# Feed-forward part of an encoder step: sums of x1 on VectorE alone, weight rounding on ScalarE, and another bank for the second half product

## The chip, the cores and the metric

One core of a Trainium2 chip runs the whole program in one launch. The metric is the device time of that launch in microseconds, as the median of several runs. Beside the plain runs one execution was recorded by the hardware profiler; its rows are quoted below. Engines go by the names of the profile: PE (TensorE), DVE (VectorE), ACT (ScalarE), POOL (GpSimd), SP (SyncE, which issues the DMAs).

## The reference, cut to what matters

One layer of a streaming encoder: four parallel token mixers, an output projection with a layer norm, and a gated convolutional feed-forward part. Prompt (1024 tokens) and sample (64 tokens) share the weights. D_MODEL is 1024, D_FF 2048, everything in float32. The change lies in the last five lines of the layer:

```python
x1 = layer_norm(DN_ALPHA * x + jnp.einsum('btd,de->bte', mix, w_out), ln1_g, ln1_b)
gate_pre = jnp.einsum('btd,df->btf', x1, w_ff_gate)
up = jnp.einsum('btd,df->btf', x1, w_ff_up)
ffn = jnp.einsum('btf,fd->btd', jax.nn.gelu(gate_c) * up, w_ff_down)
x2 = layer_norm(DN_ALPHA * x1 + ffn, ln2_g, ln2_b)
```

Here `gate_c` is a causal depthwise convolution of width 3 over `gate_pre`.

## The kernel before

**Arithmetic.** Each float32 operand is split into a rounded high part and the low part that the rounding leaves (`wh`, `wl` of a weight; `x1h`, `x1l` of x1). A product of two such operands is three matmuls: high by high, high by low, low by high. The 1088 tokens stand in three chunks of 384, 384 and 320 columns; D_MODEL is cut into 8 blocks of 128 rows. A weight tile has 128 rows of 1024 values: one output block of 128 features with its 8 blocks of input.

**Weights.** `wissue` (L246) walks a fixed plan of weight tiles: SP loads the raw tile `wr` (2 buffers), POOL rounds it to `wh` (L258, 3 buffers), DVE subtracts for `wl` (L259, 3 buffers). `wget(key, ahead)` and `pair` ask for tiles some places ahead of their use.

**Order.** The program is written out stage by stage, and a scheduler places every instruction in one fixed list for each engine from the order of the code, the tiles' dependencies and its own estimates. On the chip each engine takes its list from the front, and waits for what the next instruction needs.

**Stages around the change.** The mixers and the output projection come first. Stage F ends with two plain gate tiles (features 0 and 1: `ff_gate` calls `dense`, L308), their convolution with gelu (`conv`, L1561), and two plain up tiles (L1606 to L1608, chunks in the order 1, 0, 2, in the bank kind m), each of which multiplies the convolved gate in place (`put_up`, L1551).

Stage G does features 2 to 15 in seven steps. Each has a pair of gate tiles, two convolutions and a pair of up tiles. A pair goes through `pair` (L347): the 2 by 2 block product of two weight tiles with chunks 0 and 1 is done with seven instead of eight block products, from sums of weight blocks and sums of x1 blocks. `xsums` (L319) makes the sums of x1 once, ahead of the seven steps: it first rebuilds 24 blocks of x1 as high plus low (`whole`, POOL, L328), DVE takes differences (L337 to L339 and L344), ACT rounds each result (L332) and DVE subtracts for the low part (L333). `wsums` (L266) makes the weights' sums for each pair: `st` on DVE, rounded to `sh` by POOL (L281), low part `sl` by DVE (L282).

Within a pair, PE does in turn: product 1 (a11 by b11) in half `u` of a wide bank of kind s; product 2 (a12 by b21) in a bank of kind d; the third chunk of the first tile (`rest`, d); products with sums s2 and s1 (`u` and `v`, the wide bank's halves); the third chunk of the second tile (d); and three further products onto `u` and `v`. `kept` (L370) has ACT copy `u` to SBUF where a later product goes on adding to it; `add` adds such a copy to a result on DVE. In `up_pair` the sum then multiplies the convolved gate on POOL (L1590). Tile kinds s, d and m have two PSUM buffers each.

Stage H is the down projection: three groups of three token tiles, each over 16 weights, with a layer norm per token tile (`norm1` to `norm3`, of which L1497 is the last addition).

Of the kernel before, what the change touches and what calls it, by code (L numbers as in the profile page):

```python
# [9 lines left out]
F32 = mybir.dt.float32  # L10
# [9 lines left out]
P = 128  # L20
# [48 lines left out]
def trunk_kernel(ctx: ExitStack, tc: tile.TileContext, I, O, dbg=None):  # L69
# [39 lines left out]
    def nm(s):  # L109
        uid[0] += 1  # L110
        return f"{s}_{uid[0]}"
# [134 lines left out]
    def wissue(upto, pin=False):  # L246
        while wptr[0] <= min(upto, len(plan) - 1):
            key, ap, a = plan[wptr[0]]
            pool = wide["f"] if key[0] == "fd" and key[1] > 2 and key[1] % 2 == 0 else wp
            raw = pool.tile([P, a, 1024 // a], F32, tag="wr", name=nm("wr"), bufs=2)  # L250
            pinned(SP.dma_start(raw, ap), pin)
            if key[0] == "out" and (key[1] == 1 or key[2] == 3):
                h = slot([P, a, 1024 // a], F32R, "woh")
                l = slot([P, a, 1024 // a], F32R, "wol")
            else:
                h = pool.tile([P, a, 1024 // a], F32R, tag="wh", name=nm("wh"), bufs=3)
                l = pool.tile([P, a, 1024 // a], F32R, tag="wl", name=nm("wl"), bufs=3)
            G.tensor_scalar(h, raw, 1.0, 1.0, OP.mult, OP.mult)  # L258
            V.tensor_sub(l, raw, h.bitcast(F32))  # L259
            wtiles[key] = (h, l)  # L260
            wraw[key] = raw
            wptr[0] += 1
            if key in pairs:
                wsums(wraw.pop(pairs[key]), wraw.pop(key), key)

    def wsums(ra, rb, key):  # L266

        a11, a12, a21, a22 = ra[:, 0:4, :], ra[:, 4:8, :], rb[:, 0:4, :], rb[:, 4:8, :]
        out = []
        for j in range(2):  # L270
            h = wide["w"].tile([P, 2, 4, P], F32R, tag="sh", name=nm("sh"))
            l = wide["w"].tile([P, 2, 4, P], F32R, tag="sl", name=nm("sl"))
            t = wide["w"].tile([P, 2, 4, P], F32, tag="st", name=nm("st"), bufs=1)
            if j == 0:
                V.tensor_tensor(t[:, 0], a21, a22, OP.add)
                V.tensor_tensor(t[:, 1], t[:, 0], a11, OP.subtract)
            else:
                V.tensor_tensor(t[:, 0], a11, a21, OP.subtract)
                V.tensor_tensor(t[:, 1], a12, a22, OP.subtract)
                V.tensor_tensor(t[:, 1], t[:, 1], t[:, 0], OP.add)  # L280
            G.tensor_scalar(h, t, 1.0, 1.0, OP.mult, OP.mult)  # L281
            V.tensor_sub(l, t, h.bitcast(F32))  # L282
            out += [(h[:, 0], l[:, 0]), (h[:, 1], l[:, 1])]
        wtiles["sums", key] = out
# [32 lines left out]
    xs = {}  # L317

    def xsums():  # L319


        for j in (0, 1, 3):
            xs[j] = tuple(wide["x"].tile([P, 4, 384], F32R, tag=f"x{j}{i}", name=nm("xs"), bufs=1) for i in range(2))
        xs[2] = tuple(t[1][:, 0:4, :] for t in (xh, xl))

        def whole(c, k, eng):
            t = wide["p"].tile([P, 384], F32, tag="xf", name=nm("xf"), bufs=4)
            eng.tensor_tensor(t, xh[c][:, k, :].bitcast(F32), xl[c][:, k, :].bitcast(F32), OP.add)  # L328
            return t

        def parts(j, k, t):
            S.activation(xs[j][0][:, k, :], t, AF.Copy)  # L332
            V.tensor_sub(xs[j][1][:, k, :], t, xs[j][0][:, k, :].bitcast(F32))  # L333

        for k in range(4):
            t, b12, b22, b21 = [whole(c, kk, G) for c, kk in ((0, k), (1, k), (1, k + 4), (0, k + 4))]
            V.tensor_tensor(t, b12, t, OP.subtract)  # L337
            V.tensor_tensor(b22, b22, t, OP.subtract)
            V.tensor_tensor(b21, b21, b22, OP.subtract)  # L339
            for j, v in ((0, t), (1, b22), (3, b21)):  # L340
                parts(j, k, v)
        for k in range(4):
            b12, b22 = whole(1, k, G), whole(1, k + 4, G)
            V.tensor_tensor(b22, b22, b12, OP.subtract)  # L344
            parts(2, k, b22)

    def pair(ka, kb, add, put):  # L347

# [25 lines left out]
        u, v = two[:, 0:384], two[:, 512:896]  # L374
        product(u, a11, b11, True)
        yield
        ps = bank("d")[:, 0:384]
        product(ps, a12, b21, True)
        add(0, 0, ps, kept(u))
        yield  # L380
# [1205 lines left out]
    def up_pair(f):  # L1586
        def add(i, n0, ps, other):
            cv = cvs[f + i][:, n0:n0 + 384]
            V.tensor_tensor(other, ps, other, OP.add)  # L1589
            G.tensor_tensor(cv, cv, other, OP.mult)  # L1590
            SP.dma_start(h_d[n0 // 384][:, f + i, :], cv)
        run(pair(("fu", f), ("fu", f + 1), add, lambda i, n0, n, ps: put_up(f + i, n0, n, ps)))

# [9 lines left out]
    next(fg1)  # L1603
    xsplit(acc[7], 7)
    run(fg0, fg1)
    for f in range(2):  # L1606
        conv(f)
        run(dense(("fu", f), lambda c, n0, n, ps: put_up(f, n0, n, ps), "m", (1, 0, 2), 2 - f))  # L1608
    slot_pool(7, "x", "w", "p")
    phase("G")  # L1610
    xsums()
# [68 lines left out]
    for g, grp in enumerate(TGRP):  # L1680
# [11 lines left out]
        for f in range(16):  # L1692
            if f % 8 == 0 and (g, f // 8) not in hcur:
                hcur[g, f // 8] = h_tiles(g, f // 8)
            hi, lo = hcur[g, f // 8]
            wd = wget(("fd", 16 * g + f), 4)
            if f == 0:
                hcur[g, 1] = h_tiles(g, 1)
            if last and f >= 12:
# [67 lines left out]
```

## Time and profile before

| what | us |
|---|---|
| median of 3 runs | 2191.51 |
| lowest, highest run | 2190.42, 2193.58 |
| the profiled execution, its own time | 2194.01 |
| span of the profiled execution | 2192.3 |

In the profiled execution DVE was busy for 55% of the span, ACT for 26%, POOL for 24%; the mean granted clock of PE was 0.990 of full speed. How to read the rows: matmuls are pipelined, so that the record of one (0.33 us for 384 columns) is longer than the time from its start to the next one's start; that pitch is what a matmul costs in a row. "[0.73 <-DVE pp L1589]" means that the engine stood for 0.73 us until DVE's instruction of line 1589, which wrote `pp`, was done. Releasers are inferred by the profile.

### The profile page before, as it was taken

The page shows a single profiled execution, that of the slowest core. Times are in us where ns is not written, and L with a number is a line of the kernel's source. Part 1 is how long each engine was busy: PE and PEld are TensorE (multiplying, and loading weights), DVE is VectorE, ACT ScalarE, POOL GpSimd, SP SyncE. Part 2 cuts the span into 40 slices and gives each one's busy share as a digit, 9 for nine tenths or more (in the row PEclk, how much of TensorE's full clock was granted, in tenths as well). Part 3 has the DMA queues.
Part 4 walks back from the last instruction along what each step waited for, and adds up shares of the span by engine and source line. Part 5 has one row for each costly group of instructions (what it writes and reads, how often), then busy time and mean ns, then how long its engine had stood idle before and what let it go on. Part 6 is the DMA issues. An engine that isn't in the chain of part 4 may idle for free.

```text
span 2192.3 us, 32005 instructions
## 1 busy us (share of the span) xinstructions
PE 2115.8 (97%) x13035; PEld 1964.9 (90%) x13035; DVE 1195.2 (55%) x2137; ACT 573.8 (26%) x1113; POOL 531.6 (24%) x465
## 2 busy tenths in 40 slices
PE   8999999999999999999999999999996999999997
PEld 7999998889899888888999999997896999998886
DVE  4643345666433557645331245454659867676665
ACT  3753023444210244333101222210222111112110
POOL 1111001111123312210230111132426322224443
PEclk9999999999999999999999999999997999999998
DMA  5112321111143232131431111324211222227643
GB/s 149 52 59 90 100 63 30 53 44 42 46 149 121 78 100 79 51 99 50 139 129 52 59 51 53 123 80 149 91 66 42 59 87 72 78 91 268 223 176 111
DMA packets 193231, 200.31 MB, mean 91 GB/s; under 512 B 14588, under 2 KB 165448, under 8 KB 193084
## 3 DMA queue, kind: packets, MB, share of 16 engines
q1 hardware_dynamic: 193084, 198.26, 28.0%
q8 instruction: 103, 1.69, 0.3%
q14 instruction: 44, 0.36, 0.1%
HBM read 154.80 MB, written 43.43 MB: 90 GB/s over the span
## 4 chain that ended last, share of the span: by engine, by line
PE 80%; DVE 13%; issue 5%; POOL 2%; ACT 1%; DMA 0%; SPq 0%; DVEq 0%; POOLq 0%; ACTq 0%
PE psd L293 15%; PE psd L295 14%; PE psd L294 14%; PE pss L360 6%; PE pss L1677 3%; PE psm L293 3%; PE psm L295 3%; PE psm L294 3%; DVE wl L259 2%; DVE cv L1568 2%; PE psm L1109 2%; PE psd L1677 1%; PE psm L1677 1%; PE pss L294 1%; PE psm L1134 1%
## 5 line engine op out<-in xcount | busy, mean ns | idle before, releaser
L293 PE MATMUL psd<-xh,wh 128*128 128x384 f32 (+1 forms) x1920 | 644.1, 335 | 1.0 <-ACT xh L178 0.9
L295 PE MATMUL psd<-xh,wl 128*128 128x384 f32 (+1 forms) x1920 | 632.6, 329 | 0.0
L294 PE MATMUL psd<-xl,wh 128*128 128x384 f32 (+1 forms) x1920 | 631.2, 329 | 0.5 <-DVE xl L179 0.5
L258 POOL TENSOR_SCALAR wh<-wr 128x1024 fp32r<-128x1024 f32 x179 | 208.5, 1166 | 1052.4 <-PE psd L294 318.3
L259 DVE TENSOR_TENSOR wl<-wr,wh 128x1024 fp32r<-128x1024 f32 x179 | 262.5, 1471 | 318.9 <-POOL wh L258 302.1
L293 PEld LDWEIGHTS psd<-xh,wh 128*128 128x128 f32 x1920 | 363.7, 189 | 7.8 <-issue 3.0
L294 PEld LDWEIGHTS psd<-xl,wh 128*128 128x128 f32 x1920 | 362.5, 189 | 1.9 <-DVE xl L179 0.9
L295 PEld LDWEIGHTS psd<-xh,wl 128*128 128x128 f32 x1920 | 362.4, 189 | 0.5 <-DVE wl L259 0.3
L674 ACT ACTIVATE th<-psd,bhalf 128x384 f32<-128x384 f32 (+1 forms) x96 | 53.9, 563 | 344.2 <-PE psd L295 343.5
L293 PE MATMUL psm<-yh,wh 128*128 128x384 f32 (+1 forms) x384 | 126.5, 331 | 7.7 <-DVE th L709 7.7
L295 PE MATMUL psm<-yh,wl 128*128 128x384 f32 (+1 forms) x384 | 126.2, 329 | 0.0
L294 PE MATMUL psm<-yl,wh 128*128 128x384 f32 (+1 forms) x384 | 126.0, 328 | 0.0
L709 DVE SCALAR_TENSOR_TENSOR th<-th,psm 128x384 f32<-128x384 f32 (+1 forms) x96 | 50.3, 529 | 108.8 <-PE psm L295 107.6
L293 PE MATMUL psd<-x1h,wh 128*128 128x320 f32 (+1 forms) x272 | 85.9, 316 | 5.3 <-DVE pp L1589 4.4
L295 PE MATMUL psd<-x1h,wl 128*128 128x320 f32 (+1 forms) x272 | 84.9, 312 | 0.0
L294 PE MATMUL psd<-x1l,wh 128*128 128x320 f32 (+1 forms) x272 | 84.8, 312 | 0.0
L293 PEld LDWEIGHTS psm<-yh,wh 128*128 128x128 f32 x384 | 72.3, 188 | 10.4 <-DVE th L709 9.9
L1172 DVE CUSTOM_DVE_ANT_0 Pt<-pss,fcb 128x128 f32<-128x128 f32 (+7 forms) x64 | 48.1, 751 | 55.1 <-PE pss L1167 54.6
L711 POOL TENSOR_TENSOR th<-th,prev 128x1088 f32<-128x1088 f32 x24 | 60.9, 2536 | 58.4 <-DVE th L709 54.1
L294 PEld LDWEIGHTS psm<-yl,wh 128*128 128x128 f32 x384 | 72.5, 189 | 0.0
L295 PEld LDWEIGHTS psm<-yh,wl 128*128 128x128 f32 x384 | 72.5, 189 | 0.0
L1148 POOL TENSOR_SCALAR q<-fq 64x256 fp32r<-64x256 f32 x64 | 36.8, 575 | 131.1 <-PE pss L1162 79.6
(534 smaller groups left out, 3948.7 us busy)
## 6 DMA issues: line engine op xcount, KB each, us to landing
wr<-in_w_in_dram SPq DMA_DIRECT2D x48, 512.0 KB
wr<-in_w_ff_down_dram SPq DMA_DIRECT2D x48, 512.0 KB
wr<-in_w_mg_dram SPq DMA_DIRECT2D x32, 512.0 KB
mx_d<-th SPq DMA_DIRECT2D x24, 544.0 KB
prev<-mx_d SPq DMA_DIRECT2D x24, 544.0 KB
wr<-in_w_br_dram SPq DMA_DIRECT2D x16, 512.0 KB
wr<-in_w_ff_gate_dram SPq DMA_DIRECT2D x16, 512.0 KB
wr<-in_w_ff_up_dram SPq DMA_DIRECT2D x16, 512.0 KB
```

The source lines that it names most:

```text
L258: G.tensor_scalar(h, raw, 1.0, 1.0, OP.mult, OP.mult)
L259: V.tensor_sub(l, raw, h.bitcast(F32))
L293: PE.matmul(ps, wh, mh, start=i == 0, stop=False)
L294: PE.matmul(ps, wh, ml, start=False, stop=False)
L295: PE.matmul(ps, wl, mh, start=False, stop=i == n - 1)
L360: PE.matmul(ps, w[:, k, :], x[:, k, :], start=start and k == 0 and i == 0, stop=k == 3 and i == 2, skip_group_check=not start)
L674: S.activation(th[:, n0:n0 + n], ps, AF.Tanh, bias=b, scale=0.5)
L709: V.scalar_tensor_tensor(th[:, n0:n0 + n], th[:, n0:n0 + n], 1.0, ps[:, :n], OP.add, OP.mult)
L711: G.tensor_tensor(th, th, prev, OP.add)
L1109: PE.transpose(p3[0:sw, j, 0:w], Pt[:, s0:s0 + sw], ident[0:w, 0:w])
L1172: V.tensor_tensor_reduce(Pt[:, 0:L].rearrange("p (b n) -> p b n", b=nb), ps.rearrange("p (b n) -> p b n", b=2)[:, 0:nb, 0:n], cbs[hh][:, 0 ...
L1677: PE.matmul(ps[hf], a[:, f % 8, o:o + P], w[:, 0, sl], start=f == 0 and i == 0, stop=f == 15 and i == (2 if tt < 8 else 1))
```

## The change

1. `xsums`: the blocks of x1 are rebuilt on DVE, 16 in place of 24, since one loop makes all four results of a round and blocks are no longer rebuilt twice; the scratch `xf` has five buffers.
2. `wissue`: weights of the feed-forward gate and up projections are rounded by ACT. `wsums`: the sums are rounded by ACT too. Down weights stay on POOL.
3. `pair`: product 2 goes to a bank of kind m.
4. `up_pair`: the multiplication goes from POOL to DVE.
5. The two plain up tiles: chunk 1 of both, then chunks 0 and 2 of the first, then of the second.
6. Stage H: in the last group weights are asked for five places ahead in place of four.

```diff
-            G.tensor_scalar(h, raw, 1.0, 1.0, OP.mult, OP.mult)
+            if key[0] in ("fg", "fu"):
+                S.activation(h, raw, AF.Copy)
+            else:
+                G.tensor_scalar(h, raw, 1.0, 1.0, OP.mult, OP.mult)
             V.tensor_sub(l, raw, h.bitcast(F32))
...
-            G.tensor_scalar(h, t, 1.0, 1.0, OP.mult, OP.mult)
+            S.activation(h, t, AF.Copy)
             V.tensor_sub(l, t, h.bitcast(F32))
...
-        def whole(c, k, eng):
-            t = wide["p"].tile([P, 384], F32, tag="xf", name=nm("xf"), bufs=4)
-            eng.tensor_tensor(t, xh[c][:, k, :].bitcast(F32), xl[c][:, k, :].bitcast(F32), OP.add)
-            return t
-
-        def parts(j, k, t):
-            S.activation(xs[j][0][:, k, :], t, AF.Copy)
-            V.tensor_sub(xs[j][1][:, k, :], t, xs[j][0][:, k, :].bitcast(F32))
-
         for k in range(4):
-            t, b12, b22, b21 = [whole(c, kk, G) for c, kk in ((0, k), (1, k), (1, k + 4), (0, k + 4))]
+            t, b12, b22, b21 = [wide["p"].tile([P, 384], F32, tag="xf", name=nm("xf"), bufs=5) for _ in range(4)]
+            for v, c, kk in ((t, 0, k), (b12, 1, k), (b22, 1, k + 4), (b21, 0, k + 4)):
+                V.tensor_tensor(v, xh[c][:, kk, :].bitcast(F32), xl[c][:, kk, :].bitcast(F32), OP.add)
             V.tensor_tensor(t, b12, t, OP.subtract)
+            V.tensor_tensor(b12, b22, b12, OP.subtract)
             V.tensor_tensor(b22, b22, t, OP.subtract)
             V.tensor_tensor(b21, b21, b22, OP.subtract)
-            for j, v in ((0, t), (1, b22), (3, b21)):
-                parts(j, k, v)
-        for k in range(4):
-            b12, b22 = whole(1, k, G), whole(1, k + 4, G)
-            V.tensor_tensor(b22, b22, b12, OP.subtract)
-            parts(2, k, b22)
+            for j, v in ((0, t), (1, b22), (3, b21), (2, b12)):
+                S.activation(xs[j][0][:, k, :], v, AF.Copy)
+                V.tensor_sub(xs[j][1][:, k, :], v, xs[j][0][:, k, :].bitcast(F32))
...
-        ps = bank("d")[:, 0:384]
+        ps = bank("m")[:, 0:384]
         product(ps, a12, b21, True)
...
-            G.tensor_tensor(cv, cv, other, OP.mult)
+            V.tensor_tensor(cv, cv, other, OP.mult)
...
+    fu = []
     for f in range(2):
         conv(f)
-        run(dense(("fu", f), lambda c, n0, n, ps: put_up(f, n0, n, ps), "m", (1, 0, 2), 2 - f))
+        fu.append(dense(("fu", f), lambda c, n0, n, ps, f=f: put_up(f, n0, n, ps), "m", (1, 0, 2), 2 - f))
+        next(fu[f])
+    run(*fu)
...
-            wd = wget(("fd", 16 * g + f), 4)
+            wd = wget(("fd", 16 * g + f), 5 if last else 4)
```

The change moves instructions in the engines' lists at many places; three of them follow. Line numbers of the changed kernel are up to seven lower or three higher than those of before.

**DVE in the sums of x1.** Before, the last rounds of `xsums`: each row of `xf` from `xf` is a difference of blocks that POOL has rebuilt, each row of `xs` a low part, and the weight sum's low part `sl` stands ahead of the last four low parts (`x1l` is used again for the third sum).

```order
L333 TENSOR_TENSOR xs_2342_15177<-xf_2359_15233,xs_2341_15176 128x384
L339 TENSOR_TENSOR xf_2362_15239<-xf_2362_15239,xf_2361_15237 128x384
L333 TENSOR_TENSOR xs_2344_15179<-xf_2361_15237,xs_2343_15178 128x384
L344 TENSOR_TENSOR xf_2364_15252<-xf_2364_15252,xf_2363_15250 128x384
L333 TENSOR_TENSOR xs_2346_15181<-xf_2362_15239,xs_2345_15180 128x384
L282 TENSOR_TENSOR sl_2377_15291<-st_2378_15292,sh_2376_15290 128x1024
L333 TENSOR_TENSOR x1l_2215_14012<-xf_2364_15252,x1h_2214_14011 128x384
```

Now, in the second and third of four rounds: L332 is DVE's own rebuilding of a block, L333 to L336 are the differences, L339 the low parts.

```order
L332 TENSOR_TENSOR xf_2354_15205<-x1h_2212_14009,x1l_2213_14010 128x384
L333 TENSOR_TENSOR xf_2351_15202<-xf_2352_15203,xf_2351_15202 128x384
L332 TENSOR_TENSOR xf_2355_15222<-x1h_2212_14009,x1l_2213_14010 128x384
L334 TENSOR_TENSOR xf_2352_15203<-xf_2353_15204,xf_2352_15203 128x384
L339 TENSOR_TENSOR xs_2342_15177<-xf_2351_15202,xs_2341_15176 128x384
L335 TENSOR_TENSOR xf_2353_15204<-xf_2353_15204,xf_2351_15202 128x384
L339 TENSOR_TENSOR x1l_2215_14012<-xf_2352_15203,x1h_2214_14011 128x384
L336 TENSOR_TENSOR xf_2354_15205<-xf_2354_15205,xf_2353_15204 128x384
L339 TENSOR_TENSOR xs_2344_15179<-xf_2353_15204,xs_2343_15178 128x384
L332 TENSOR_TENSOR xf_2356_15223<-x1h_2214_14011,x1l_2215_14012 128x384
L339 TENSOR_TENSOR xs_2346_15181<-xf_2354_15205,xs_2345_15180 128x384
```

The rebuilding has come into DVE's list, four rows in each round, and the first weight sum stands behind all four rounds.

**PE at the third chunk of a pair's second tile**, in the up pair of features 4 and 5 (d bank, matmuls of 320 columns). In square brackets stands the engine whose work the row waits for. Before:

```order
L360 MATMUL pss_2478_16106<-x1l_2213_14010,wh_2446_15891 128x384
L360 MATMUL pss_2478_16106<-x1h_2212_14009,wl_2447_15892 128x384
L360 MATMUL pss_2478_16106<-x1h_2212_14009,wh_2446_15891 128x384
L293 MATMUL psd_2462_16000<-x1h_2216_14013,wh_2428_15700 128x320 [waits DVE_49]
L294 MATMUL psd_2462_16000<-x1l_2217_14014,wh_2428_15700 128x320
L295 MATMUL psd_2462_16000<-x1h_2216_14013,wl_2429_15701 128x320
```

Now:

```order
L354 MATMUL pss_2449_15900<-xs_2341_15176,sh_2422_15688 128x384
L354 MATMUL pss_2449_15900<-xs_2342_15177,sh_2422_15688 128x384
L354 MATMUL pss_2449_15900<-xs_2341_15176,sl_2423_15689 128x384
L296 MATMUL psd_2454_15984<-x1h_2216_14013,wh_2420_15684 128x320 [waits PE_49]
L297 MATMUL psd_2454_15984<-x1l_2217_14014,wh_2420_15684 128x320
L298 MATMUL psd_2454_15984<-x1h_2216_14013,wl_2421_15685 128x320
```

The first matmul of the third chunk waited for a DVE instruction, the add that reads the d bank of product 2. Now it waits only for PE's own earlier work.

**ACT in the same pair.** Before, its list holds the copies of PSUM (`pp`, `gp`) and the gelus (`cv`):

```order
L370 ACTIVATE pp_2442_15840<-pss_2436_15719 128x384
L1547 ACTIVATE gp_2423_15689<-pss_2436_15719 128x384
L370 ACTIVATE pp_2459_15942<-pss_2457_15916 128x384
L1573 ACTIVATE cv_2443_15869<-cv_2443_15869 128x1088
L1573 ACTIVATE cv_2444_15879<-cv_2444_15879 128x1088
L370 ACTIVATE pp_2461_15998<-pss_2457_15916 128x384
L370 ACTIVATE pp_2463_16039<-pss_2457_15916 128x384
```

Now:

```order
L364 ACTIVATE pp_2451_15926<-pss_2449_15900 128x384
L284 ACTIVATE sh_2425_15695<-st_2427_15697 128x1024
L259 ACTIVATE wh_2441_15881<-wr_2440_15879 128x1024
L1567 ACTIVATE cv_2435_15853<-cv_2435_15853 128x1088
L364 ACTIVATE pp_2453_15982<-pss_2449_15900 128x384
L1567 ACTIVATE cv_2436_15863<-cv_2436_15863 128x1088
L284 ACTIVATE sh_2443_15885<-st_2445_15887 128x1024
L364 ACTIVATE pp_2455_16023<-pss_2449_15900 128x384
```

Roundings of weight tiles (`wh`, L259) and of weight sums (`sh`, L284) stand between the copies of `pss` and the gelus.

## Rows read from the trace of the kernel before

**Rows 1.** The page, part 1: busy us (share of the span) xinstructions of each engine
```profile
PE 2115.8 (97%) x13035; PEld 1964.9 (90%) x13035; DVE 1195.2 (55%) x2137; ACT 573.8 (26%) x1113; POOL 531.6 (24%) x465
```

**Rows 2.** Windows: length, busy us (xcount) of PE, PEld, DVE, ACT, POOL, PEclk, DMA
```profile
1660.00:1680.00 20.00, 6.39 (x21) 6.39 (x22) 20.00 (x20) 4.57 (x10) 16.36 (x13) 0.57 0.00 0
...
1900.00:1950.00 50.00, 49.26 (x298) 48.04 (x297) 35.20 (x52) 6.55 (x13) 14.15 (x13) 1.00 0.24 71
```

**Rows 3.** Waits from 1560 us on: who <- for whom, us in total, times, longest
```profile
POOL wh L258 <- PE pss L360: 54.1, 11, 8.1
...
PE psd L293 <- DVE pp L1589: 4.4, 6, 0.8
```

**Rows 4.** Timeline of DVE, 1645 to 1673: start, duration, engine, line, operation, tiles, xcount
```profile
1645.09 0.49 DVE L1553 TENSOR_TENSOR cv<-cv,psm 128x320 f32<-128x320 f32 x1 [2.96 <-PE psm L295]
...
1669.81 0.54 DVE L344 TENSOR_TENSOR xf<-xf,xf 128x384 f32<-128x384 f32 x1
1670.28 1.34 DVE L333 TENSOR_TENSOR xs<-xf,xs 128x384 fp32r<-128x384 f32 x1
1671.55 2.01 DVE L282 TENSOR_TENSOR sl<-st,sh 128x1024 fp32r<-128x1024 f32 x1
```

**Rows 5.** Timeline of PE, 1653 to 1697, with [idle before <-releaser]
```profile
1653.34 0.42 PE L293 MATMUL psd<-x1h,wh 128*128 128x320 f32 x1 [0.24 <-ACT gp L1549]
...
1673.61 0.69 PE L360 MATMUL pss<-xs,sl 128*128 128x384 f32 x1 [16.49 <-DVE sl L282]
...
1680.01 0.34 PE L360 MATMUL pss<-xs,sl 128*128 128x384 f32 x1
...
1684.36 0.69 PE L360 MATMUL pss<-x1h,sl 128*128 128x384 f32 x1 [0.92 <-DVE sl L282]
...
1696.95 0.33 PE L360 MATMUL psd<-x1h,wl 128*128 128x384 f32 x1
1697.12 0.31 PE L293 MATMUL psd<-x1h,wh 128*128 128x320 f32 x1
```

**Rows 6.** Tile xf: duration in ns (minimum/median/maximum), first and last start, forms
```profile
L328 POOL TENSOR_TENSOR xf<-x1h,x1l x24: 1005/1260/1979, 1634.1 to 1678.1; 128x384 f32<-128x384 f32 x24
...
L333 DVE TENSOR_TENSOR xs<-xf,xs x12: 1343/1346/1395, 1648.6 to 1670.3; 128x384 fp32r<-128x384 f32 x12
```

**Rows 7.** Groups of ACT by form: busy us, mean ns | idle before
```profile
L693 ACT ACTIVATE yh<-yr 128x1088 fp32r<-128x1088 f32 x12 | 13.1, 1109 | 11.5 <-DMA yr<-y_d 11.5
```

**Rows 8.** Timeline of DVE, down projection
```profile
2139.44 4.62 DVE L259 TENSOR_TENSOR wl<-wr,wh 128x1024 fp32r<-128x1024 f32 x4
```

**Rows 9.** Tile wr, 1675 to 1700: durations in ns, first and last start
```profile
L258 POOL TENSOR_SCALAR wh<-wr x3: 1070/1563/1984, 1684.5 to 1698.0; 128x1024 fp32r<-128x1024 f32 x3
...
L251 SPq DMA_DIRECT2D wr<-in_w_ff_up_dram x2: 384/456/527, 1680.2 to 1680.7; - x2
```

**Rows 10.** Timeline of PE, first up pair and two steady steps
```profile
1712.52 0.34 PE L360 MATMUL psd<-x1h,wh 128*128 128x384 f32 x1
1715.05 0.61 PE L360 MATMUL pss<-xs,wh 128*128 128x384 f32 x2 [2.20 <-DVE pp L1589]
...
1842.50 0.34 PE L360 MATMUL pss<-x1h,wh 128*128 128x384 f32 x1
1843.57 0.41 PE L293 MATMUL psd<-x1h,wh 128*128 128x320 f32 x1 [0.73 <-DVE pp L1589]
1843.82 0.31 PE L294 MATMUL psd<-x1l,wh 128*128 128x320 f32 x1
...
1888.63 0.41 PE L293 MATMUL psd<-x1h,wh 128*128 128x320 f32 x1 [0.73 <-DVE pp L1589]
```

**Rows 11.** Timeline of PE, last group of the down projection
```profile
2137.37 0.39 PE L1677 MATMUL psd<-wh,hh 128*128 128x512 f32 x1
2140.70 0.79 PE L1677 MATMUL psd<-wl,hh 128*128 128x512 f32 x1 [2.94 <-DVE wl L259]
...
2143.98 0.39 PE L1677 MATMUL psm<-wh,hl 128*128 128x512 f32 x1
```

## The prediction

> **What bounds the kernel now.** I read the page first: TensorE (PE) is busy for 97% of the span [rows 1]. So only places where PE stands, or runs at a low granted clock, can give time back; faster work on VectorE (DVE), ScalarE (ACT) or GpSimd (POOL) is worth something only there. Second, windows [rows 2]: in the steady pair loop PE is busy for 49.26 of 50 us; in the 20 us from 1660, where the sums of x1 are made, for 6.39 at a granted clock of 0.57. Third, the waits of PE from 1560 to the end: they come down to low parts of the weight sums (L282), the add of L1589, seven times, of which six are of one kind [rows 3], and a down weight's low part (L259). That is the list this change can act on. Fourth, the timelines of PE and DVE show where each of these waits stands.
>
> **Place 1: sums of x1.** *Before.* DVE evicts the last plain tile at 1645.09 and works on sums until the low part that PE needs, which begins at 1671.55 and takes 2.01 [rows 4]. PE starts again at 1673.61, after 16.49 idle [rows 5]. DVE's operations explain the length: a 384-column one that begins at 1669.81 is followed by the next 0.47 later, but the next takes 1.34 [rows 4]. The twelve L333 for xs have a median of 1346 ns, and POOL's 24 adds, of 1260 each, fill the same stretch [rows 6]. So these twelve alone lose some 0.8 each, about 10 us, to work beside them.
> PE then runs 24 matmuls from 1673.61 to about 1680.3, 6.7 us where a pitch of 0.17 (1696.95 to 1697.12) makes 4.2, and waits again, until the second weight sum's low part comes at 1684.36. By 1697.12, when it takes the up weight's third chunk, it has done 84 matmuls of 384 columns since the long wait [rows 5].
> *After.* POOL's adds are gone. By the order DVE has 48 operations of 384 columns behind the same eviction: 16 sums, 16 differences, 16 low parts. From 1645.5, at 0.47 each, that is 22.6 us. In the first round DVE needs ACT's fourth rounding, which stands behind the copy of a PE tile; before, PE went on behind that copy at 1653.34 [rows 5]. That is 2 us later than DVE would be there, so the sums end near 1670.3. Two weight-sum operations and the gate's add take 1.7. ACT rounds 1024 columns in 1.04 (1109 ns for 1088 [rows 7]), the low part takes 1.15 (four in 4.62 [rows 8]), and PE starts near 1674.6, 1 us *later* than before. But the second weight sum now follows directly: three operations of 0.61, ACT's 1.04 and the low part end near 1678.8, against 1684.3. The 24 matmuls, 6.7 us as before, last until 1681.3, so it is there when PE comes. The up weight must have landed and been rounded too: its buffer is free near 1676.3, from SP's issue to the first rounding it was 4.2 us [rows 9], with 1.04 for the rounding that makes 1681.5. The sixty other matmuls at 0.1735 end near 1691.8. **Gain 1697.1 - 1691.8 = 5.3.** Bounds: 0, if something other than POOL makes DVE slow, and 8, if ACT is not waited for and PE's slow spell gets shorter.
>
> **Place 2: first up pair.** PE stops after 1712.52 and goes on at 1715.05 behind L1589's add [rows 10]: 2.53, less one pitch 2.36. The second product now has a bank of another kind (m, two buffers, one use in a pair), and the tile after it does not wait for that add. **Gain 2.4**, bounds 0 (DVE is late for everything there) and 2.4.
>
> **Place 3: six steady up pairs.** PE goes from 1842.50 to 1843.57 and on to 1843.82 [rows 10]. Against pitches of 0.17 and 0.15 this loses 0.9 and 0.1. Before, three tiles of a pair share two d buffers, and the third waits for the add that empties the first. After, two share them, and in the order the third chunk waits for PE's own past work alone. **Gain 6 x 1.0 = 6.0**; bounds 3 (half is lost to a later wait for one of ACT's copies) and 9 (other short waits go as well).
>
> **Place 4: down projection.** PE goes from 2137.37 to 2140.70 for a low part; ten matmuls, by the program's order, take until 2143.98, 6.6 us, where a pitch of 0.23 makes 2.3 [rows 11]. On DVE that low part stands behind a layer norm's operations and begins, with three more, at 2139.44 [rows 8]. Issued one step earlier in the last group, it stands ahead of them. **Gain 4.3**; bounds 0 (the next weight, needed 3.6 us later, waits in its place) and 4.3.
>
> **What is moved at no gain.** Rounding of 32 feed-forward weights and of 28 weight sums goes to ACT: 60 x 1.04 = 62 us, some 8 in a step of 45, where ACT is busy for 6.55 of 50 [rows 2]. The cover is ACT's idle time; without it a PSUM copy behind a rounding is late by 1.04. The multiply of L1590 goes to DVE, 21 x 0.47 = 10 us, in a loop where DVE is busy for 35.20 of 50 [rows 2]; it is not ahead of anything that PE waits for. The plain up tiles take the second chunk first, but DVE's order has all sums behind the last eviction, so I count nothing; SP only starts one weight of the last group sooner.
>
> **Sum.** 5.3 + 2.4 + 6.0 + 4.3 = 18.0. The profiled execution took 2194.0, of which 2192.3 is the span; 2194.0 - 18.0 = 2176.0. The median of the three runs is 2191.5, 2.5 below the profiled one, so the forecast is **2173.5**.
>
> **Rivals.**
> *A, the sums gain nothing on DVE.* For it: by my own sum PE's start after the long wait is not earlier, and DVE gets 16 operations more, 7.5 us. Against it: the 0.47 and the 1.34 of neighbours of one size [rows 4]. Place 1 then gives 0 and the time is 2173.5 + 5.3 = 2178.8; if place 4 stays too, 2183. Chance 0.22.
> The Trainium skill bears on this (Perfetto Trace Analysis, "Optimizing Scalar/DVE Operations"): GpSimd and VectorE share an SBUF read port, it says, so that moving work between these two might not help. By that rule place 1 gives 0. The trace speaks against it here, as far as the long L333 stand beside POOL's adds: a move that ends POOL's part ends the sharing.
> *B, more than the sum.* A step takes 45.06 from one such wait to the next (1843.57, 1888.63 [rows 10]); its 168 matmuls of 384 columns at 0.1735 and 96 of 320 at 0.147 make 43.3. Of the 1.7 between I took 1.0. The rest, six times, is 4, and a slow spell one or two us shorter in place 1 makes it 6 in all: 2167. For it: less collides. Against: some of these are short waits for ACT's copies, which get more company. Chance 0.12.
> *C, slower: ACT is held at the head of its queue.* A weight's rounding waits for a buffer that PE empties. On POOL these waits are 54.1 us in 11, up to 8.1 [rows 3], and nothing that PE needs stands behind them. On ACT the copies of L370 do, and the next product into the same bank waits for such a copy. It decides from 18 us over 13 pairs, 1.4 a pair. If one pair in two loses the mean of 4.9, that is 6.5 x 4.9 = 32 and the time 2205. Against it: in the order, a rounding that waits for PE waits for a tile ahead of the product whose copy stands behind it. Chance 0.07.
> *D, no change to be seen,* because the edit does not do what it says (the adds go, but a dependency on ACT keeps DVE as long) and the steps give back what the bank gains: 2191. Chance 0.08.
>
> **How the numbers follow.** The forecast itself has 0.51, 2171 to 2177. The three runs of before lie 3 us apart; 0.2%, 4.4 us, is about what can be told from no change. Faster by more than that: forecast, A and B, 0.85; same 0.08; slower 0.07. The range holds the forecast, most of B below and A with place 4 lost above, 2165 to 2184; it leaves out C, D and the ends of A and B.
>
> **What would show it.** Right: DVE operations of 0.47 pitch in the sums and none of 1.3; a long wait of PE of about 18 us, and none for the second weight sum; the up weight's third chunk at about 1692; no wait of PE for the add in the steps, and a step near 44; no wait of 2.9 near the end. Wrong: operations of 1.3 without POOL beside them (A), PE waiting for L364 behind a rounding (C), or PE waiting for another low part in the last group (place 4).

## The result, and the profile after

| kernel | median of the runs, us | lowest, highest | ratio to before, 95% interval |
|---|---|---|---|
| before | 2192.55 (4 runs) | 2190.42, 2193.58 | |
| changed | 2170.03 (4 runs) | 2168.34, 2172.70 | 0.990 (0.988 to 0.992) |

The change takes 22.5 us off by these medians; 18.0 had been forecast, from a lower median of before. 2170.0 lies in the stated range of 2165 to 2184, and below the 2171 to 2177 of the forecast itself, about halfway to rival B's 2167. The profiled execution of the changed kernel took 2169.9 us. The page, span and part 1, against [rows 1]:

```profile
span 2168.2 us, 31902 instructions
...
PE 2105.0 (97%) x13035; PEld 1957.4 (90%) x13035; DVE 1170.2 (54%) x2174; ACT 633.8 (29%) x1173; POOL 410.6 (19%) x360
```

PE has 10.8 us less busy time for the same 13035 matmul records, so a part of the gain is time at a low clock. POOL lost 121 us of work, ACT has 60 more. DVE has 37 instructions more and is busy for 25 us less. The windows of [rows 2] again (length, busy us of PE, PEld, DVE, ACT, POOL, granted clock, DMA):

```profile
1660.00:1680.00 20.00, 11.28 (x47) 10.46 (x48) 16.42 (x35) 7.69 (x12) 0.00 (x0) 0.65 0.20 52
...
1900.00:1950.00 50.00, 50.00 (x299) 49.03 (x298) 32.72 (x54) 16.40 (x24) 1.05 (x1) 1.00 0.25 77
```

In the 20 us from 1660, PE is busy for 11.28 where it was 6.39 (in part because the changed kernel is 5 us ahead by then); in the steady loop it has no gap left, POOL is all but idle, and ACT is busy for 16.4 of 50 instead of 6.6. The waits of PE from 1560 on, the whole list:

```profile
PE pss L354 <- ACT sh L284: 17.0, 1, 17.0
PE psd L1674 <- DVE wl L262: 0.6, 1, 0.6
PE psd L296 <- DVE x1l L189: 0.6, 1, 0.6
PE pss L354 <- ACT wh L259: 0.3, 1, 0.3
PE pss L354 <- DVE sl L285: 0.3, 1, 0.3
```

The waits for DVE's add, seven before ([rows 3] has six), are gone; so is the one of 2.94 near the end [rows 11]. One long wait is left, for the sums.

The span fell by 24.1. To see where, I took marks on PE's timeline that both kernels have: the first matmul of the first pair, the first third-chunk matmul (320 columns) of the first up pair and of the next gate pair, the step (the mean of four, from one gate pair's third chunk to the next's, features 6 to 14), and the tail from the last up pair's third chunk to the end. The same marks stand in this table for every run, since they tell more than totals that differ by 2 or 3 us from execution to execution.

| run | rounding | bank | sums of x1 | first matmul at | a: to first up pair's third chunk | b: on to next gate pair's | step | tail | median, us |
|---|---|---|---|---|---|---|---|---|---|
| before | POOL | d | POOL | 1644.9 | 52.2 | 24.4 | 45.06 | 223.3 | 2192.6 |
| changed | ACT | m | DVE | 1639.8 | 46.8 | 21.8 | 43.94 | 218.0 | 2170.0 |
| e1 bank back | ACT | d | DVE | 1640.6 | 46.9 | 22.3 | 44.15 | 218.9 | 2174.1 |
| e2 bank alone | POOL | m | POOL | 1642.0 | 52.2 | 24.4 | 45.61 | 222.9 | 2192.7 |
| e3 sums back | ACT | m | POOL | 1640.9 | 48.3 | 21.9 | 43.95 | 218.0 | 2171.2 |
| e4 POOL beside the sums | ACT | m | DVE | 1641.6 | 64.5 | 21.8 | 43.93 | 218.0 | 2189.8 |
| e5 rounding back | POOL | m | DVE | 1639.2 | 48.5 | 23.6 | 45.04 | 217.8 | 2179.2 |
| e6 multiplication back | ACT | m | DVE | 1638.8 | 46.9 | 21.8 | 43.98 | 218.1 | 2170.3 |
| e7 four ahead | ACT | m | DVE | 1638.4 | 46.9 | 21.8 | 43.94 | 221.0 | 2172.2 |
| e8 early weight sums | ACT | m | DVE | 1641.9 | a + b: 64.5 | | 43.95 | 218.0 | 2166.7 |
| e9 rounding alone | ACT | d | POOL | 1644.4 | 48.7 | 22.8 | 44.21 | 221.9 | 2180.8 |
| e10 sums on PE | ACT | m | PE | 1639.2 | 41.8 | 21.8 | 43.94 | 218.0 | 2165.0 |
| e11 POOL in the steps | ACT | m | DVE | 1640.4 | 46.8 | 21.8 | 50.50 | 219.4 | 2201.2 |

Of the 24.1, the stretches a and b give 5.4 and 2.6, the steps up to the last up pair 5.7 (247.4 to 241.8), the tail 5.3: 19.0 in all. The other 5.1 lie ahead of the first matmul of the first pair, nearly all of it ahead of 1500 us, where the order is the same on every engine. Most of it, 4.5, is one wait and the slow spell behind it (a stretch at the lower granted clock) that this profiled execution of before had (PE's waits, 300 to 400):

```profile
PE psm L949 <- DVE vt L953: 3.4, 1, 3.4
```

It is 3.4 in the profile of e9 too, and 1.5 in the changed kernel and all other runs, e2 among them, with the same instructions there. So it is put down to the execution, not to the change, which leaves the change some 19 us by the marks.

### The profile page after: what moved, and what is told of

It reads as the page before. It is cut to its first block, busy times and chain, and to the rows that moved or that the text cites. A ratio compares the mean times of both kernels' runs of the same rounds, so it can differ in the third digit from the quotient of the medians.

```text
span 2168.2 us, 31902 instructions
## 1 busy us (share of the span) xinstructions
PE 2105.0 (97%) x13035; PEld 1957.4 (90%) x13035; DVE 1170.2 (54%) x2174; ACT 633.8 (29%) x1173; POOL 410.6 (19%) x360
## 3 DMA queue, kind: packets, MB, share of 16 engines
q1 hardware_dynamic: 193084, 198.26, 28.4%
## 4 chain that ended last, share of the span: by engine, by line
PE 81%; DVE 8%; issue 6%; POOL 2%; DMA 1%; ACT 1%; SPq 0%; DVEq 0%; POOLq 0%; ACTq 0%
PE psd L296 14%; PE psd L298 14%; PE psd L297 14%; PE pss L354 8%; PE pss L1674 3%; PE psm L296 3%; PE psm L297 3%; PE psm L298 3%; DVE wl L262 2%; PE psd L1674 1%; PE psm L1674 1%; PE psm L354 1%; PE pss L297 1%; PE pss L298 1%; PE pss L296 1%
## 5 line engine op out<-in xcount | busy, mean ns | idle before, releaser
L261 POOL TENSOR_SCALAR wh<-wr 128x1024 fp32r<-128x1024 f32 x147 | 170.8, 1164 | 1244.4 <-PE pss L354 364.3
L259 ACT ACTIVATE wh<-wr 128x1024 fp32r<-128x1024 f32 x32 | 34.0, 1061 | 144.9 <-PE psd L297 46.9
L354 PE MATMUL pss<-xs,sh 128*128 128x384 f32 x224 | 59.1, 345 | 17.0 <-ACT sh L284 17.0
```

Of the source, the lines that this page charges most:

```text
L259: S.activation(h, raw, AF.Copy)
L354: PE.matmul(ps, w[:, k, :], x[:, k, :], start=start and k == 0 and i == 0, stop=k == 3 and i == 2, skip_group_check=not start)
```

## The experiments

Ratios are to runs of the kernel before that were made beside each experiment; their medians were 2190.2, 2190.4, 2190.9 and 2193.2.

**e1, the bank back.** In `pair`:

```diff
-        ps = bank("m")[:, 0:384]
+        ps = bank("d")[:, 0:384]
```

> The changed kernel, but the second half product is back in a bank of kind d. My theory: the bank alone gives places 2 and 3, so the time rises by about 2.6 + 6.7 = 9 us over the changed kernel: the stretch from the first up pair's third chunk to the next gate pair's goes from 21.8 back to about 24, a step from 43.9 back to about 45, and the waits of PE for the add come back, some 0.7 each. Rival: the steps got shorter because DVE and POOL collide less, not because of the bank; then a step stays at 43.9 to 44.2 and the time rises by less than 3 us.

Measured: 2174.1, a step of 44.15 and not 45. PE's waits of the kind that the bank was to take away, in all steps:

```profile
PE psd L296 <- DVE pp L1583: 0.6, 1, 0.6
PE psd L296 <- ACT gp L1543: 0.6, 1, 0.6
```

One wait of 0.6 is left of six times 0.73 [rows 3], with the old bank. The theory falls, and the rival's step came: not the bank took the wait away. The time rose by 4.1, more than the rival's 3. By the marks the bank is worth 0.2 us a step, 0.5 in stretch b and 0.9 in the tail, about 2.5 in all.

**e2, the bank alone.** The reverse edit in the kernel before.

> The kernel before, with the bank of kind m for the second half product and nothing else. My theory: gain of 8 to 9 us on the kernel before (2184), a step of about 44, no wait of PE for the add of L1589; the sums stretch stays at 48 us and the wait of 2.9 near the end stays. Rival (the roundings and the multiplication on POOL also hold PE): a step stays over 44.5, gain under 5 us.

Measured: 2192.7, ratio 1.0006 (0.9996 to 1.0015): no gain, and a step is longer, 45.61. PE's waits there:

```profile
PE pss L360 <- DVE pp L1589: 9.6, 6, 2.2
PE psd L1677 <- DVE wl L259: 3.6, 2, 3.0
```

The first of the six is the first pair's, 2.20 as before [rows 10], so the bank alone does not give place 2 either. The other five are 1.48 or 1.49 each, where the steady pairs had 0.73 before, and stand at another add of the same line:

```profile
1848.20 0.61 PE L360 MATMUL pss<-xs,wh 128*128 128x384 f32 x2 [1.48 <-DVE pp L1589]
```

```profile
1847.59 0.55 DVE L1589 TENSOR_TENSOR pp<-pss,pp 128x384 f32<-128x384 f32 x1
```

Before, PE waited for the add that empties the bank of product 2 (`pp<-psd,pp`). With another bank the third chunk stands seven matmuls earlier in PE's list, and PE is held at DVE's next add, the one on the wide bank (`pp<-pss,pp`). DVE was behind; the bank only chose at which add PE met it.

**e3, the sums back on POOL.** `xsums` as before, all else as in the changed kernel.

> The changed kernel, but the sums of x1 as before (24 adds on POOL, the third sum in a loop of its own). My theory: POOL's adds make DVE's two-input operations 1.35 us long again, the stretch from the first pair's third chunk to the up pair's goes from 42.6 to about 48, the time rises by 5 to 6 us. Rival A (the sums gain nothing on DVE; the 5.4 us of that stretch come from the rounding on ACT or the order of the weight sums): the stretch stays within 1.5 us of 42.6.

Measured: 2171.2; a is 48.3, 1.5 more than changed. This falls to the rival, whose bound was 1.5. POOL's adds do stretch DVE's low parts (1346 ns as in [rows 6]), but in DVE's list the first weight sum's low part now stands in the first round (at 1645.53), where before it stood behind all four rounds of the first loop [rows 4], and PE does single products between the sums; its waits:

```profile
PE pss L363 <- ACT xs L335: 6.4, 3, 2.6
PE pss L363 <- DVE xs L336: 4.2, 3, 1.8
PE pss L363 <- ACT sh L284: 2.7, 1, 2.7
```

**e4, POOL beside the sums.** In the loop of `xsums`; the added results are used by nothing:

```diff
+        z = slot(s="z")
...
                 S.activation(xs[j][0][:, k, :], v, AF.Copy)
+                if j != 2:
+                    for kk in (k, k + 4):
+                        G.tensor_tensor(z[:, 0:384], xs[j][0][:, k, :].bitcast(F32), xh[0][:, kk, :].bitcast(F32), OP.add)
```

> The changed kernel with 24 useless adds of 384 columns on POOL beside the sums; DVE, ACT and PE have the same lists as in the changed kernel, and nothing waits for the adds. My theory: each DVE operation that runs beside such an add takes about 1.35 instead of 0.55 us, some 0.8 us for each of 20 or so, so that PE's long wait grows from 17 to 29 to 36 us and the time by 12 to 19. Rival (the 1.35 us of before came from something else than POOL, such as the operands): DVE's operations stay at 0.55 and the time does not move.

Measured: 2189.8, 19.8 slower (the theory had 12 to 19); a grows by 17.7, and PE's long wait doubles. The lists of PE, DVE and ACT are those of the changed kernel, entry by entry. DVE's operations on tile xf (ns, minimum/median/maximum), and PE's wait:

```profile
L343 DVE TENSOR_TENSOR xs<-xf,xs x12: 547/1344/1418, 1645.5 to 1682.7; 128x384 fp32r<-128x384 f32 x12
...
L336 DVE TENSOR_TENSOR xf<-xf,xf x4: 546/950/1343, 1646.0 to 1677.2; 128x384 f32<-128x384 f32 x4
```

```profile
PE pss L358 <- ACT sh L284: 34.7, 1, 34.7
```

Nearly all of the change's gain is lost to adds that nothing waits for. The stretching is by operand. In the kernel before, DVE's timeline beside one of POOL's roundings:

```profile
1681.34 0.54 DVE L1581 TENSOR_TENSOR gp<-psd,pp 128x384 f32<-128x384 f32 x1
1681.80 1.14 DVE L333 TENSOR_TENSOR x1l<-xf,x1h 128x384 fp32r<-128x384 f32 x1
```

```profile
1681.50 1.04 POOL L281 TENSOR_SCALAR sh<-st 128x1024 fp32r<-128x1024 f32 x1 [2.17 <-DVE st L280]
```

Both rows of DVE overlap it. The add with one input in PSUM takes 0.54, its usual time; the low part with both inputs in SBUF 1.14, and not 0.55. From 1600 us on, 24 such adds of 384 columns with an input in PSUM overlap an instruction of POOL by 0.1 us or more; the longest takes 0.56. The Trainium skill (SBUF — State Buffer, "Who interferes with whom") says so: a VectorE instruction with two SBUF inputs contends with a GpSimd one that reads SBUF, through a shared read interface. The trace agrees, at 0.8 us an operation of 384 columns.

**e5, the rounding back on POOL.** Both roundings of part 2 undone. My theory for the steps had changed after e1 and e2, and the expectation says to what.

> The changed kernel, but feed-forward weights and weight sums are rounded on POOL again; sums on DVE, bank m, multiplication on DVE stay. After the runs on the bank my theory for the steps is changed: a step got shorter because POOL's roundings no longer stretch DVE's operations beside them, so that DVE's add is in time; the bank only decides at which tile PE waits. Then a step goes from 43.9 back to 45 or more (the bank alone gave 45.6), PE waits for DVE's add L1583 again, and the time rises by 8 to 12 us. Rival (the multiplication's move off POOL is what counts): a step stays under 44.3. The recorded theory had no gain from this part at all: a rise under 2 us.

Measured: 2179.2, 9.2 over the changed kernel; a step 45.04, b 23.6, a 48.5, and PE waits for the add again (6.4 in six). The new theory holds, the recorded one falls. The order of DVE in one step, from the convolution to the late add, first with rounding on POOL:

```profile
1776.97 0.88 DVE L1556 TENSOR_SCALAR cv<-gp,pk 128x1024 f32<-128x1024 f32 x1
...
1780.81 3.27 DVE L1559 SCALAR_TENSOR_TENSOR cv<-gp,pk,cv 128x1024 f32<-128x1024 f32 x2
...
1789.50 0.61 DVE L1550 COPY gp<-pk 128x2 f32<-128x2 f32 x1
...
1793.59 0.55 DVE L1580 TENSOR_TENSOR pp<-pss,pp 128x384 f32<-128x384 f32 x1
```

and POOL's roundings in that time:

```profile
1781.97 1.05 POOL L258 TENSOR_SCALAR wh<-wr 128x1024 fp32r<-128x1024 f32 x1 [4.67 <-PE psd L294]
1788.88 1.20 POOL L281 TENSOR_SCALAR sh<-st 128x1024 fp32r<-128x1024 f32 x1 [5.87 <-DVE st L276]
```

and the same rows of DVE with rounding on ACT (changed kernel):

```profile
1773.80 0.81 DVE L1559 TENSOR_SCALAR cv<-gp,pk 128x1024 f32<-128x1024 f32 x1
...
1777.58 2.48 DVE L1562 SCALAR_TENSOR_TENSOR cv<-gp,pk,cv 128x1024 f32<-128x1024 f32 x2
...
1785.47 0.16 DVE L1553 COPY gp<-pk 128x2 f32<-128x2 f32 x1
...
1788.54 0.55 DVE L1583 TENSOR_TENSOR pp<-pss,pp 128x384 f32<-128x384 f32 x1
```

From the first convolution's start to the add it is 16.6 us in one and 14.7 in the other: the second convolution's pair takes 3.27 and not 2.48, beside `wh`; a copy of two columns 0.61 and not 0.16, beside `sh`; and one weight-sum operation of 0.6 has been placed ahead of the add.

**e6, the multiplication back on POOL.**

```diff
-            V.tensor_tensor(cv, cv, other, OP.mult)
+            G.tensor_tensor(cv, cv, other, OP.mult)
```

> The changed kernel, but the multiplication of up_pair is on POOL again. My theory: some 10 us of DVE work less, three POOL operations a step more that collide with DVE; PE has slack for both, a step stays at 43.9 to 44.2, the time moves by less than 2 us. Rival (the multiplication on POOL is what made DVE late): a step of 44.6 or more, 4 to 8 us slower.

Measured: 2170.3, step 43.98, every mark from the first matmul on as in the changed kernel within 0.2. Part 4 is worth nothing here.

**e7, four weights ahead.**

```diff
-            wd = wget(("fd", 16 * g + f), 5 if last else 4)
+            wd = wget(("fd", 16 * g + f), 4)
```

> The changed kernel, but weights of the last group are asked for four places ahead again. My theory: PE's wait near the end for a down weight's low part goes from 0.6 back to 2.9, with a slow spell after it: 4 us slower, all behind the pair loop. Rival (that wait went because of other changes, since a run with the sums on POOL and one with the bank back keep 0.7 there): no wait over 1 us, same time within 1 us.

Measured: 2172.2, 2.2 slower by the medians; the tail is 3.0 longer, the wait is back:

```profile
2119.62 0.50 PE L1674 MATMUL psd<-wl,hh 128*128 128x512 f32 x1 [2.95 <-DVE wl L262]
2119.96 0.39 PE L1674 MATMUL psm<-wh,hh 128*128 128x512 f32 x1
2120.19 0.40 PE L1674 MATMUL psm<-wl,hh 128*128 128x512 f32 x1
```

It costs 3.0 and not 4.3, since PE goes on at full clock here (0.34 to the next matmul, then 0.23).

**e8, weight sums ahead of the sums of x1.**

```diff
     phase("G")
+    wissue(wpos["fg", 3])
     xsums()
```

> The changed kernel with one line more: the first pair's weights are asked for ahead of the sums of x1, so that their weight sums stand ahead of the four rounds in DVE's list, in time that DVE has idle while PE does the plain up tiles. In the run with the sums on POOL the weight sums stood there, and PE could begin with single products in between. My theory: PE's products need x1's sums alone and start some 3 us earlier, the stretch from the first pair's third chunk to the up pair's goes from 42.6 to about 39, and the time falls by 3 to 4 us. Rival (DVE's work before the sums grows by as much as falls away behind them, as DVE is the bound there): the stretch within 1 us of 42.6.

Measured: 2166.7 (ratio to before 0.989, 0.988 to 0.991). a + b is 64.5 against 68.6: 4.1 less. The third chunk of the up pair is split into two there, so a alone can't be read. The theory holds.

**e9, the rounding alone.** Part 2 in the kernel before, nothing else.

> The kernel before, with the rounding of feed-forward weights and weight sums on ACT and nothing else: bank d, sums and multiplication on POOL as before. Theory after the runs so far: the rounding's move is what shortens the steps (roundings on POOL stretch convolutions, small copies and low parts on DVE ahead of the add that PE waits for), so a step goes from 45.1 to 44.2 or less, as in the run with the bank back; the stretch of the sums gets shorter by 2 to 4 us, since the weight sums no longer pass through POOL's queue behind its adds; the wait of 2.9 near the end stays. In all 9 to 13 us faster than before, where the recorded prediction would have 0. Rival (it takes rounding on ACT and the bank together): a step of 44.8 or more, gain under 6 us.

Measured: 2180.8, 10.0 faster than before. A step is 44.21, b 22.8, a 48.7; the wait near the end stays. The theory holds, and with e2 it is the cross of both: rounding on ACT with the old bank shortens a step by 0.85, the new bank with rounding on POOL by nothing. In the sums something else moved with it: as in e3, DVE's list has the first weight sum's low part in the first round (at 1649.08). How much of the 3.5 in stretch a comes from that place in the list, and how much from the rounding itself, no run parts.

**e10, sums on PE.** On top of e8, the sums as products with plus and minus identity:

```diff
+        one = [wide["p"].tile([P, P], F32R, tag=f"i{i}", name=nm("one"), bufs=1) for i in range(2)]
+        S.activation(one[0], ident, AF.Copy)
+        S.activation(one[1], ident, AF.Copy, scale=-1.0)
         for k in range(4):
...
+            for j, add, sub in ((0, (b12,), (b11,)), (1, (b22, b11), (b12,)), (3, (b21, b12), (b22, b11)), (2, (b22,), (b12,))):
+                ps = bank("dm"[j % 2])[:, 0:384]
+                terms = [(w, t[c][:, kk, :]) for w, bs in zip(one, (add, sub)) for c, kk in bs for t in (xh, xl)]
...
+                S.activation(xs[j][0][:, k, :], ps, AF.Copy)
+                V.tensor_sub(xs[j][1][:, k, :], ps, xs[j][0][:, k, :].bitcast(F32))
```

> The changed kernel with the weight sums ahead of the sums of x1, and these sums made by PE in its idle time: plus and minus identity times the parts, 22 matmuls of 384 columns a round, 88 in all, into PSUM, rounded by ACT from there; DVE is left with 16 low parts. It tests that the stretch is DVE's 48 operations and nothing else. If so, PE has 88 x 0.1735 = 15.3 us of work in place of 17 us of waiting and a slow spell, and runs on at the full clock: the stretch from the first pair's third chunk to the up pair's goes from 42.6 to 36 to 38 (39 to 40 in the run with early weight sums), no PE wait over 3 us there, time 2163 to 2166. Rival (ACT and the eviction of 16 PSUM tiles through two kinds of banks become the bound, 1 us or more per tile and its round trip): the stretch is 40 or more, and the time no better than with early weight sums alone.

Measured: 2165.0 (ratio to before 0.988, 0.987 to 0.990), a + b 63.6, 5.0 less than changed. The mark of the expectation, the first pair's third chunk, moved behind the new matmuls; from the first product instead, a went from 46.8 to 41.8. Windows:

```profile
1640.00:1660.00 20.00, 20.00 (x117) 19.78 (x116) 16.06 (x31) 11.10 (x20) 0.00 (x0) 1.00 0.23 62
1660.00:1680.00 20.00, 20.00 (x121) 19.44 (x120) 7.51 (x15) 6.17 (x12) 0.00 (x0) 1.00 0.20 53
```

PE is busy for all of the 40 us that held its longest wait, at full clock, with 88 matmuls more: with 32 of DVE's 48 operations gone PE waits for nothing there. But of the 5.0, 4.1 came with the line of e8 alone, so this does not show that DVE's 48 operations and nothing else made the stretch. Against e8 the medians differ by 1.7, which the intervals do not part; the marks give 0.9. That is all that the identity products add here, since PE's waiting is filled with 15 us of new work. The median is the lowest of the kernels run.

**e11, POOL in the steps.** Behind each rounding on ACT, from feature 6 on, the call of

```diff
+    def beside(h):
+        z = wide["p"].tile([P, 384], F32, tag="xf", name=nm("z"), bufs=5).rearrange("p (a b) -> p a b", a=3)
+        for _ in range(2):
+            G.tensor_tensor(z, h.bitcast(F32), h.bitcast(F32), OP.add)
```

> The changed kernel with two useless adds of 384 columns on POOL behind each rounding of a weight or weight sum from feature 6 on, some 16 a step; ACT still does the rounding, the lists of PE, DVE and ACT are those of the changed kernel, and nothing waits for the adds. It parts the two ways in which rounding on POOL can make DVE's add late: by stretching DVE's operations beside it, or by being late itself (POOL's queue, its trip to DVE). If it is the stretching, DVE's convolutions and low parts in a step get longer by 2 to 4 us together, and a step goes from 43.9 to 44.5 or more, with PE waits for L1583 again. If it is lateness, a step stays at 43.9 to 44.1.

Measured: 2201.2, slower than before (ratio 1.004, 1.003 to 1.005); a step of 45.9 first, then 50.5 in the mean: 6.6 more than changed, of which 4.1 is one wait of PE and most of the rest the slow spell behind it. The convolution's large operation on DVE in one step (busy, mean ns), here, then in the changed kernel, and PE's waits:

```profile
L1571 DVE SCALAR_TENSOR_TENSOR cv<-gp,pk,cv 128x1024 f32<-128x1024 f32 x4 | 6.7, 1701 | 0.0
```

```profile
L1562 DVE SCALAR_TENSOR_TENSOR cv<-gp,pk,cv 128x1024 f32<-128x1024 f32 x4 | 5.0, 1279 | 0.0
```

```profile
PE pss L363 <- DVE pp L1592: 18.7, 6, 4.1
```

The lists of PE, DVE and ACT are again those of the changed kernel, entry by entry. So stretching alone, with ACT rounding as early as ever, makes the add late by up to 4.1. That it is also what held PE in the steady steps of the kernel before, its own trace shows: DVE from PE's last gate product to the add that PE waits for at 1843.57 [rows 10], and POOL's rounding in the middle of that time.

```profile
1831.78 0.56 DVE L1581 TENSOR_TENSOR gp<-pss,pp 128x384 f32<-128x384 f32 x1 [0.82 <-PE pss L360]
...
1836.22 3.28 DVE L1568 SCALAR_TENSOR_TENSOR cv<-gp,pk,cv 128x1024 f32<-128x1024 f32 x2
...
1842.97 0.54 DVE L1589 TENSOR_TENSOR pp<-psd,pp 128x384 f32<-128x384 f32 x1
```

```profile
1837.37 1.05 POOL L258 TENSOR_SCALAR wh<-wr 128x1024 fp32r<-128x1024 f32 x1 [4.68 <-PE psd L294]
```

Between these rows DVE is never idle for more than 0.04 us, so it waits for no result of POOL, and lateness of POOL has no share in this add. The thirteen operations ahead of the add take 11.2 us; the same thirteen take 10.3 in the changed kernel (from 1773.20 to 1783.53 there) and 13.7 in e11. The convolution's pair, 3.28 and not 2.48, is 0.8 of the difference. PE comes to the third chunk 10.9 us after the first of these rows (one pitch behind 1842.50 [rows 10]). The add is over after 11.7; without the stretching it would be over after 10.9, just in time (an estimate from these rows). In e9 PE's list also leaves 0.2 more for it. For the later add of e2 POOL is late as well: DVE stands 0.95 for its `sh` on the way there.

Part 5 was not tried by itself; the plain stage, from the first gate tile's third chunk to the first pair, takes 30.6 us in both kernels, so it shows nothing to explain.

## Why the prediction was right in its sum and wrong in its parts

**Place 1, forecast 5.3, measured 5.4.** The schedule worked out for the changed kernel is what the profile shows. DVE, with the columns of [rows 4]:

```profile
1640.01 0.49 DVE L1547 TENSOR_TENSOR cv<-cv,psm 128x320 f32<-128x320 f32 x1 [2.96 <-PE psm L298]
1640.41 1.96 DVE L332 TENSOR_TENSOR xf<-x1h,x1l 128x384 f32<-128x384 f32 x4
...
1648.65 0.56 DVE L339 TENSOR_TENSOR xs<-xf,xs 128x384 fp32r<-128x384 f32 x1 [2.06 <-ACT xs L338]
...
1664.84 0.55 DVE L339 TENSOR_TENSOR xs<-xf,xs 128x384 fp32r<-128x384 f32 x1
...
1668.18 1.23 DVE L285 TENSOR_TENSOR sl<-st,sh 128x1024 fp32r<-128x1024 f32 x1 [0.23 <-ACT sh L284]
```

and tile xf, against [rows 6], then PE, against [rows 5]:

```profile
L332 DVE TENSOR_TENSOR xf<-x1h,x1l x16: 547/550/552, 1640.4 to 1660.8; 128x384 f32<-128x384 f32 x16
...
L339 DVE TENSOR_TENSOR xs<-xf,xs x12: 547/549/559, 1643.7 to 1664.8; 128x384 fp32r<-128x384 f32 x12
```

```profile
1668.20 1.01 PE L354 MATMUL pss<-xs,sh 128*128 128x384 f32 x2 [17.01 <-ACT sh L284]
...
1686.62 0.31 PE L296 MATMUL psd<-x1h,wh 128*128 128x320 f32 x1
```

Every sum and low part takes 0.55, the wait for ACT's fourth rounding is there (2.06 for 2 forecast), PE's long wait is 17.0 (18), the second is gone, and the third chunk comes 46.8 us behind the first matmul. As forecast, the gain lies behind the long wait and not in it: PE goes on 28.4 us behind the first matmul, where it was 28.7. Behind it the second wait is gone and its slow spell too: PE's granted clock was 0.53 from 1684.4 to 1690.0, and is 0.99 from 1674 to 1680 now.

What failed is the name of the cause: the gain was put down to the sums' move. By the table, rounding alone brings a from 52.2 to 48.7 (e9), sums on DVE with rounding on POOL (and all other parts as changed) to 48.5 (e5), both to 46.8. Each alone gives 3.5 to 3.8, and the second only 1.5 to 1.9 more, so the 5.4 can't be divided between them. Rival A, that the sums gain nothing on DVE, is wrong about the sharing of the port (e4); what they gain depends on where the rounding is. The rule of the Trainium skill that was named beside it (Perfetto Trace Analysis, "Optimizing Scalar/DVE Operations": moving work between GpSimd and VectorE might not help) would give 0. The runs give 1.5 with the rounding on ACT (e3) and up to 3.8 with it on POOL (e5), both less than the forecast's 5.3.

**Place 2, forecast 2.4, measured 2.6; place 3, forecast 6.0, measured 5.7 for the steps ahead of the last up pair.** (The last pair's own share, about 1, lies in the tail.) The sizes are right, as the row of each stall gave them; the cause is wrong. The step that failed: "After, two share them, and in the order the third chunk waits for PE's own past work alone. Gain 6 x 1.0 = 6.0". It looked at which tile PE waited for, and did not ask where the late add would be met next. With the bank alone (e2) PE is held at DVE's next add, and for longer. The lateness goes with the rounding (e5, e9), because POOL's roundings stretch DVE's work ahead of the add (e11, and the rows of before beside it).

**"What is moved at no gain".** This is the term that was mis-sized: the rounding's move was costed at nothing, and it gives 10.0 alone (e9) and 9.2 when undone (e5). Only what ACT takes on was priced, not what leaves POOL, although the price per collision, 0.8, stood in place 1. The multiplication was costed at nothing and is nothing (e6).

**Place 4, forecast 4.3, measured 3.0 (e7).** The wait of 2.9 went; the slow spell behind it, 1.4 of the forecast, is not there every time. The tail is shorter by 5.3, since it also holds the last pair's part of place 3.

**The rivals.** C, ACT held at the head of its queue, did not come: one wait of 0.3 for `wh`, in the sums. Of B, the shorter step came in part: 43.94 where the count of matmuls makes 43.3. The sum of the parts, 19.0, is near the forecast, since the four stalls were all the stalls there were, and something in the change removed each; a right total is no evidence for the attribution. It was luck that the rounding, put at nothing, stood in the same change as the bank that was given its gain: with the bank alone the time would not have moved (e2).

## What to carry to other kernels

A stall that names a buffer can be a late producer: ask what stands ahead of that producer in its engine's list, and what stretches it, before giving the buffer the gain. When work leaves POOL, price what it did to VectorE's two-input operations beside it, not only its own time. And where an idle TensorE waits for sums made elsewhere, look first at what stands ahead of them in the list (4.1 us from one line, e8); products with an identity can make the sums too, but 88 of them added only 0.9 by the marks (e10).

## What the runs showed of the hardware that was not expected

The same wait of PE near the end, 2.94 to 2.97 us behind the same work, had two outcomes. Windows in the kernel before, the 3 us behind the wait, and in e9, the wait and the 3 us behind it; the third number from the end is the granted clock:

```profile
2140.70:2143.70 3.00, 3.00 (x7) 2.42 (x8) 3.00 (x3) 0.00 (x0) 0.00 (x0) 0.51 0.84 274
```

```profile
2127.71:2130.71 3.00, 0.06 (x1) 0.00 (x1) 3.00 (x5) 0.00 (x0) 0.00 (x0) 1.00 0.62 250
2130.71:2133.71 3.00, 3.00 (x13) 2.46 (x14) 3.00 (x3) 0.00 (x0) 0.00 (x0) 1.00 0.80 264
```

Before, PE ran on at 0.51 of full speed, the lower of its two levels (1.2 GHz) for nearly all of that time; in e9 (and e7) at 1.00, the upper one (2.4 GHz), and in e7 the wait cost 3.0 where it had cost 4.3. The run with the bank alone (e2) had a slow spell too (0.63). No run here tells what decides it. It came in two profiles of four, so a slow spell behind a short wait is better left out of a sum, or set at half.
